# Chunked gate sums, split maximum rows and ScalarE head scaling in an mLSTM and ConvFFN decoder layer

## The chip, the cores and the metric

The kernel runs as one program on one core of a Trainium2 chip. TensorE (PE in the profile; PEld is its weight load), VectorE (DVE), ScalarE (ACT), GpSimd (POOL) and SyncE (SP, which only issues DMAs here) each have an instruction stream of their own and meet at semaphores. The metric is device time in microseconds, the median of several runs; lower is better.

## The reference, cut to what matters

One decoder layer on 512 positions of width 1024: a mixer (four mLSTM heads of width 256, beside a gated convolution of width 31 with a layer norm) and a convolutional FFN of inner width 2816. The change lies in the gates of the mLSTM and in the norm of its heads. For a head, with chunks of 128 positions:

```python
lfc = jax.nn.log_sigmoid(chunks(f_pre))
b = jnp.cumsum(lf_, axis=-1)
dmat = jnp.where(causal, b[..., :, None] - b[..., None, :] + i_[..., None, :], -jnp.inf)
m_t = jnp.maximum(b + m[..., None], jnp.max(dmat, axis=-1))
scores = jnp.einsum("bhtd,bhsd->bhts", q_, k_) * jnp.exp(dmat - m_t[..., None])
...
h = num / jnp.maximum(jnp.abs(den), jnp.exp(-m_t))[..., None]
...
h = rms_norm(h, ml_norm_g[l].reshape(H, Dh)).reshape(Bsz, S, D_ML)
```

The kernel carries no state from chunk to chunk. With F the running sum of the log forget gates over all 512 positions and a = i - F, the running maximum of a over positions (not below 0) is M, and the weight of source s at target t is exp(a_s - M_t).

## The kernel before

Positions lie as NT = 4 tiles of 128, channels as KT = 8 tiles of 128. Every large product runs in three passes of type float32r, high part by high, high by low and low by high (`mm3`, lines 198 to 202), 512 columns each. `w_load` brings a weight block by an SP DMA into one of two raw buffers and splits it into a high part on ACT (line 182) and a low part on POOL (line 183).

After the gated inputs and the first value product `make_v(0)`, which also gives the gates `gz`, the stretch of the change begins. The log forget gates `lf` are computed on ACT and DVE (lines 568 to 576). On TensorE then come, in the order of the code:

- the projections `qko` 0 and 1 of head 0 (`head_proj`, 24 matmuls each; 0 and 1 give q, 2 and 3 give k, 4 and 5 the output gate `so`),
- the running sums F in bank `fcum` (line 608): for tile tt one product with the triangle `tri` and one with `ones` for each earlier tile, ten float32 products of 4 columns; DVE copies F out as `Fc` (line 610) and forms `ga` = a (line 611),
- projection 2, then `aT` (line 616): a turned to 4 rows of 512 by products with `ident`; DVE scans the running maximum into `Mr` (line 618),
- projection 3, then `mtok` (line 623): the maximum turned back to positions, used in `em` (lines 625 and 626), and `make_E(0)`,
- projections 4 and 5.

`make_E(h)` (lines 588 to 599) spreads row h of `Mr` over 128 partitions by a float32 product into bank `Mb` (line 590), adds the causal mask on DVE (`Md`, line 592) and takes seven exponentials on ACT into `E` (lines 597 and 599); three of them read `Mb` itself.

Then, for heads 0 to 2, `attention(h)` is woven with the projections of head h + 1: scores `s` (line 514), their product with `E` on DVE (line 515), outputs `o` (line 525), copied and squared on ACT into `hn` and `ssq` (lines 528 to 530), the factor `fac` on DVE and POOL (lines 535 to 541), the scaling of `hn` by `fac` on DVE (line 544: four instructions per head), and the turn `hT` of the scaled heads on TensorE (line 550), which DVE and ACT use for the parts `hh` and `hl`. `make_E(h + 1)` and the values `v` of head h + 1 stand between `o` and `hT`. The banks of `fcum`, `aT`, `mtok`, `Mb`, `s`, `o` and `hT` are two PSUM buffers used in turn (`atbank`); the second bank of `hT` of a head is thus the one that `Mb` of the next head had.

Beside all this run the 31 taps of the convolution: 25 per channel tile on DVE (`cv`, line 716), the rest on ACT and POOL, and after the last tap the blocks of the conditioning weights (`ada`: a DMA issued from ACT's queue, line 165, and a product with a sum on DVE, line 167).

TensorE and SP issue in the order of the code. On DVE, ACT and POOL a scheduler merges the streams when the program is built, from times of its own model; the taps and the `ada` blocks have the lowest priority. Once built, each engine's order is fixed.

Of the kernel before, what the change touches and what calls it, by code (L numbers as in the profile page):

```python
# [10 lines left out]
F32 = mybir.dt.float32  # L11
F32R = mybir.dt.float32r
BF16 = mybir.dt.bfloat16
AF = mybir.ActivationFunctionType
ALU = mybir.AluOpType
PSUM = bass.MemoryType.PSUM

P = 128
D = 1024
T = 512  # L20
KT = D // P
NT = T // P
H = 4
# [31 lines left out]
def decoder_layer(ctx, tc, w_glu0, x, c, adaT, vecs, w_glu, w_qko, w_v0, w_v, w_out, w_up, w_down, out):  # L55
    nc = tc.nc
    V, S, G, PE = nc.vector, nc.scalar, nc.gpsimd, nc.tensor

    const = ctx.enter_context(tc.tile_pool(name="const", bufs=1))
# [28 lines left out]
    def slot(name, dt=F32):  # L88
        return slots.tile([P, T], dt, tag="t", name=name)
# [15 lines left out]
    ident = const.tile([P, P], F32, name="ident")  # L105
    make_identity(nc, ident)
    ones = const.tile([P, P], F32, name="ones")
    V.memset(ones, 1.0)
    tri = const.tile([P, P], F32, name="tri")
# [156 lines left out]
    for tt in range(NT):  # L266
# [9 lines left out]
        if tt < NT - 1:  # L276
# [7 lines left out]
                    op0=ALU.add)  # L284
# [204 lines left out]
    def head_proj(h, i):  # L489

        pieces, qs, ks, so = heads[h]
        ps = mmbank(f"qko{h}_{i}")
        proj(ps, pieces, i * KT)
        e = 2 * h + i % 2
        if i < 2:
            qs.append(conv4(ps, e, f"q{h}_{i}"))
        elif i < 4:
            ks.append(conv4(ps, 8 + e, f"k{h}_{i}"))
        else:
            t = slot(f"so{h}_{i}")  # L500
            S.activation(t, ps, AF.Tanh, scale=0.5)
            so.append(t)
# [3 lines left out]
    def attention(h):  # L506

        _, qs, ks, so = heads[h]

        for cc in range(NT):  # L510
            n = NS[cc]
            sp = atbank(f"s{h}_{cc}")
            for d in range(2):
                PE.matmul(sp[:, :n], ks[d][:, cc * P : (cc + 1) * P], qs[d][:, cc * P :], start=d == 0, stop=d == 1)  # L514
            V.scalar_tensor_tensor(out=E[h][cc], in0=sp[:, :n], scalar=DH**-0.5, in1=E[h][cc], op0=ALU.mult, op1=ALU.mult)
            if cc % 2:
                yield
        ssq = small.tile([P, NT], F32, tag="ssq", name=f"ssq{h}")
        dm = small.tile([P, NT], F32, tag="dm", name=f"dm{h}")
        hn = [slot(f"hn{h}_{i}") for i in range(2)]  # L520
        for tt in range(NT):
            o = atbank(f"o{h}_{tt}")
            for cc in range(tt + 1):
                a = (tt - cc) * P
                PE.matmul(o[:, : DH + 2], E[h][cc][:, a : a + P], vs[h][cc], start=cc == 0, stop=cc == tt)
            junk = small.tile([P, DH], BF16, tag="junk2", bufs=2, name=f"junko{h}_{tt}")
            hv = hn[tt // 2][:, (tt % 2) * DH : (tt % 2 + 1) * DH]
            S.activation(dm[:, tt : tt + 1], o[:, DH : DH + 1], AF.Abs)
            S.activation(hv, o[:, :DH], AF.Copy)
            S.activation(junk, hv, AF.Square, accum_out=ssq[:, tt : tt + 1])  # L530
            if tt in (1, 2):
                yield
        rd = small.tile([P, NT], F32, tag="rd", name=f"rd{h}")
        fac = small.tile([P, NT], F32, tag="fac", name=f"fac{h}")
        V.tensor_tensor(out=dm, in0=dm, in1=em[:, :, h], op=ALU.max)
        V.reciprocal(rd, dm)
        V.tensor_tensor(out=ssq, in0=ssq, in1=rd, op=ALU.mult)
        V.tensor_tensor(out=ssq, in0=ssq, in1=rd, op=ALU.mult)
        V.tensor_scalar(out=ssq, in0=ssq, scalar1=1.0 / DH, scalar2=EPS, op0=ALU.mult, op1=ALU.add)
        G.tensor_tensor(out=fac, in0=ssq, in1=mhalf, op=ALU.pow)  # L540
        V.tensor_tensor(out=fac, in0=fac, in1=rd, op=ALU.mult)
        for tt in range(NT):
            hv = hn[tt // 2][:, (tt % 2) * DH : (tt % 2 + 1) * DH]
            V.tensor_scalar(out=hv, in0=hv, scalar1=fac[:, tt : tt + 1], scalar2=None, op0=ALU.mult)
        yield
        for e in range(2):
            tp = atbank(f"hT{h}_{e}")
            for tt in range(NT):
                src = hn[tt // 2][:, (tt % 2) * DH + e * P : (tt % 2) * DH + (e + 1) * P]
                PE.transpose(tp[:, tt * P : (tt + 1) * P], src, ident)  # L550
            t = so[e]
            V.scalar_tensor_tensor(out=t, in0=t, scalar=1.0, in1=tp, op0=ALU.add, op1=ALU.mult)
            hi, lo = slot(f"hh{h}_{e}", F32R), slot(f"hl{h}_{e}", F32R)
            g = ghalf[:, 2 * h + e : 2 * h + e + 1]
            S.activation(hi, t, AF.Copy, scale=g)
            last_lo[0] = V.scalar_tensor_tensor(out=lo, in0=t, scalar=g, in1=hi.bitcast(F32), op0=ALU.mult, op1=ALU.subtract)
            hy[2 * h + e] = (hi, lo)
# [8 lines left out]
    fa, fe, fu, fl, fr, lf = (g16(f"g_{i}") for i in ("fa", "fe", "fu", "fl", "fr", "lf"))  # L566
# [18 lines left out]

    E = [None] * H

    def make_E(h):
        mb = atbank(f"Mb{h}")
        PE.matmul(mb, ident[:H, h : h + 1].to_broadcast([H, P]), Mr, start=True, stop=True)  # L590
        md = slot(f"Md{h}")
        V.tensor_tensor(out=md.rearrange("p (t m) -> p t m", t=NT), in0=mb.rearrange("p (t m) -> p t m", t=NT),
                        in1=cmask[:, None, :].to_broadcast([P, NT, P]), op=ALU.add)
        E[h] = head_tiles(f"E{h}", F32)
        for cc in range(NT):
            b = ga[:, cc, h : h + 1]
            S.activation(E[h][cc][:, :P], md[:, cc * P : (cc + 1) * P], AF.Exp, bias=b, scale=-1.0)
            if cc < NT - 1:
                S.activation(E[h][cc][:, P:], mb[:, (cc + 1) * P :], AF.Exp, bias=b, scale=-1.0)
# [3 lines left out]

    fps = atbank("fcum")
    fv = fps[:, : NT * H].rearrange("p (t h) -> p t h", t=NT)
    for tt in range(NT):
        for cc in range(tt + 1):
            PE.matmul(fv[:, tt, :], tri if cc == tt else ones, lf[:, cc, :], start=cc == 0, stop=cc == tt)
    Fc, ga = g16("Fc"), g16("ga")
    V.tensor_copy(Fc, fv)  # L610
    V.tensor_tensor(out=ga, in0=gz[:, :, :H], in1=Fc, op=ALU.subtract)
    head_proj(0, 2)

    aps = atbank("aT")
    for tt in range(NT):
        PE.matmul(aps[:H, tt * P : (tt + 1) * P], ga[:, tt, :], ident, start=True, stop=True)
    Mr = const.tile([H, T], F32, name="Mr")
    V.tensor_tensor_scan(out=Mr, data0=aps[:H, :], data1=zero[:H, :].to_broadcast([H, T]), initial=0.0, op0=ALU.max, op1=ALU.max)
    head_proj(0, 3)
    mps = atbank("mtok")  # L620
    mv = mps[:, : NT * H].rearrange("p (t h) -> p t h", t=NT)
    for tt in range(NT):
        PE.matmul(mv[:, tt, :], Mr[:, tt * P : (tt + 1) * P], ident[:H, :H], start=True, stop=True)
    em = g16("em")
    V.tensor_tensor(out=em, in0=Fc, in1=mv, op=ALU.add)
    S.activation(em, em, AF.Exp, scale=-1.0)

    make_E(0)
    for i in range(4, 6):
        head_proj(0, i)  # L630


    RD = float(D) ** 0.5
# [483 lines left out]
```

## Time and profile before

| | us |
|---|---|
| median of 3 runs | 800.17 |
| lowest and highest run | 799.45, 800.42 |
| span of the profiled execution, first to last instruction | 795.9 |
| TensorE busy in it | 781.6 |
| VectorE, GpSimd, ScalarE busy | 474.5, 436.5, 380.1 |
| idle time of TensorE before the heads' turn `hT` of head 0 | 1.4 |
| idle time of TensorE before `aT` | 0.7 |

The profile is of one execution; its own time is its span and some 4.3 us around it, as far as the median tells. Rows of a timeline give start, length, engine, line, operation and tile; a bracket at the end of a row is the idle time ahead of it and what ended that. Lengths overlap, since an engine starts the next instruction before the last has left it; the distance of two starts is what an instruction costs in a full queue.

### The profile page before, as it was taken

What the parts mean: (1) busy time and instruction counts of PE and PEld (TensorE: products, weight loads), DVE (VectorE), ACT (ScalarE), POOL (GpSimd) and SP (SyncE); (2) the same over time, 40 slices, a digit from 0 to 9 for tenths busy, and PEclk for the clock granted to TensorE, in tenths of its full rate; (3) what the DMA queues carried; (4) which work ended last, traced back from release to release, by engine and by line L of the source; (5) the groups of instructions that cost most, each with busy time, mean ns of one, the idle gap of its engine ahead of it and who ended that gap; (6) DMA issues with size and microseconds to landing.
All of it is one profiled execution on the core that took longest, in us unless ns stands there. A gap on an engine that the chain in (4) does not pass through costs nothing.

```text
span 795.9 us, 10370 instructions
## 1 busy us (share of the span) xinstructions
PE 781.6 (98%) x3786; PEld 652.2 (82%) x3786; DVE 474.5 (60%) x748; ACT 380.1 (48%) x709; POOL 436.5 (55%) x351
## 2 busy tenths in 40 slices
PE   7999999999999999999999999999999999999996
PEld 5888897777888888888889988888888888888885
DVE  6769999999996435547958794455444453000014
ACT  6684548758474454561345454444444444212212
POOL 4789759869598433442841474444454444444420
PEclk9999999999999999999999999999999999999998
DMA  8963214122037231426854652222222222222205
GB/s 326 347 243 133 81 61 153 54 105 107 28 94 250 80 133 55 159 106 235 320 187 157 218 180 106 106 75 84 106 106 106 105 90 97 107 105 106 80 0 186
DMA packets 24887, 106.97 MB, mean 134 GB/s; under 512 B 2914, under 2 KB 2946, under 8 KB 17412
## 3 DMA queue, kind: packets, MB, share of 16 engines
q1 hardware_dynamic: 16740, 83.22, 29.3%
q10 hardware_dynamic: 8096, 23.08, 8.2%
q8 instruction: 30, 0.49, 0.3%
q14 instruction: 21, 0.17, 0.1%
HBM read 102.08 MB, written 4.21 MB: 134 GB/s over the span
## 4 chain that ended last, share of the span: by engine, by line
PE 90%; DVE 5%; ACT 1%; DMA 1%; issue 1%; DVEq 0%; POOL 0%; SPq 0%; POOLq 0%; ACTq 0%
PE up L201 10%; PE up L200 10%; PE up L202 10%; PE dn L202 5%; PE dn L200 5%; PE dn L201 5%; PE qko L200 4%; PE qko L201 4%; PE qko L202 4%; PE glu L345 4%; DVE cv L716 3%; PE glu L200 2%; PE glu L201 2%; PE glu L202 2%; PE s L514 2%; PE mixa L202 2%
## 5 line engine op out<-in xcount | busy, mean ns | idle before, releaser
L716 DVE SCALAR_TENSOR_TENSOR cv<-gt,cvw,cv 128x502 f32<-128x502 f32 (+24 forms) x200 | 134.4, 725 | 1.9 <-ACT cv L704 1.3
L1043 DVE TENSOR_TENSOR fo<-dn,g2r 128x512 f32<-128x512 f32 x8 | 5.5, 692 | 100.3 <-PE dn L202 100.3
L712 POOL TENSOR_TENSOR cs<-cs,cs 128x510 f32<-128x510 f32 (+3 forms) x32 | 42.8, 1341 | 3.6 <-ACT cs L710 3.6
L183 POOL TENSOR_TENSOR wup_1024l<-wup,wup_1024h 128x512 fp32r<-128x512 f32 x20 | 27.0, 1348 | 31.8 <-ACT wup_1024h L182 31.7
L183 POOL TENSOR_TENSOR wup_1536l<-wup,wup_1536h 128x512 fp32r<-128x512 f32 x20 | 27.0, 1352 | 29.1 <-ACT wup_1536h L182 29.0
L183 POOL TENSOR_TENSOR wup_512l<-wup,wup_512h 128x512 fp32r<-128x512 f32 x20 | 26.8, 1338 | 23.4 <-ACT wup_512h L182 23.4
L183 POOL TENSOR_TENSOR wup_0l<-wup,wup_0h 128x512 fp32r<-128x512 f32 x20 | 27.2, 1358 | 20.8 <-ACT wup_0h L182 20.8
L201 PE MATMUL up<-u2l,wup_0h 128*128 128x512 f32 (+1 forms) x100 | 36.5, 365 | 0.2 <-DVE u2l L885 0.2
L200 PE MATMUL up<-u2h,wup_0h 128*128 128x512 f32 (+1 forms) x100 | 36.5, 365 | 0.0
L200 PE MATMUL up<-u2h,wup_1024h 128*128 128x512 f32 (+1 forms) x100 | 36.4, 364 | 0.0
L202 PE MATMUL up<-u2h,wup_0l 128*128 128x512 f32 (+1 forms) x100 | 36.4, 364 | 0.0
L200 PE MATMUL up<-u2h,wup_512h 128*128 128x512 f32 (+1 forms) x100 | 36.4, 364 | 0.0
L201 PE MATMUL up<-u2l,wup_512h 128*128 128x512 f32 (+1 forms) x100 | 36.4, 364 | 0.0
L202 PE MATMUL up<-u2h,wup_512l 128*128 128x512 f32 (+1 forms) x100 | 36.4, 364 | 0.0
L200 PE MATMUL up<-u2h,wup_1536h 128*128 128x512 f32 (+1 forms) x100 | 36.4, 364 | 0.0
L201 PE MATMUL up<-u2l,wup_1536h 128*128 128x512 f32 (+1 forms) x100 | 36.4, 364 | 0.0
L202 PE MATMUL up<-u2h,wup_1536l 128*128 128x512 f32 (+1 forms) x100 | 36.4, 364 | 0.0
L202 PE MATMUL up<-u2h,wup_1024l 128*128 128x512 f32 (+1 forms) x100 | 36.4, 364 | 0.0
L201 PE MATMUL up<-u2l,wup_1024h 128*128 128x512 f32 (+1 forms) x100 | 36.3, 363 | 0.0
L167 DVE SCALAR_TENSOR_TENSOR junk<-ada,cb 128x1024 bf16<-128x1024 f32 x20 | 32.6, 1631 | 6.3 <-DMA ada<-in_adaT 6.2
L183 POOL TENSOR_TENSOR wqko_1024l<-wqko,wqko_1024h 128x512 fp32r<-128x512 f32 x12 | 16.6, 1380 | 25.8 <-PE v L201 15.1
L183 POOL TENSOR_TENSOR wd_1024l<-wd,wd_1024h 128x512 fp32r<-128x512 f32 x11 | 14.3, 1296 | 29.8 <-ACT wd_1024h L182 29.8
(727 smaller groups left out, 2617.0 us busy)
## 6 DMA issues: line engine op xcount, KB each, us to landing
wup<-in_w_up SPq DMA_DIRECT2D x22, 1024.0 KB, 4.8
wqko<-in_w_qko SPq DMA_DIRECT2D x12, 1024.0 KB, 4.7
wd<-in_w_down SPq DMA_DIRECT2D x11, 1024.0 KB, 4.8
ada<-in_adaT ACTq DMA_DIRECT2D x20, 512.0 KB, 5.6
ada<-in_adaT SPq DMA_DIRECT2D x16, 512.0 KB, 7.6
wo<-in_w_out SPq DMA_DIRECT2D x8, 1024.0 KB, 4.7
spare<-in_adaT ACTq DMA_DIRECT2D x12, 512.0 KB, 8.4
wglu<-in_w_glu SPq DMA_DIRECT2D x5, 1024.0 KB, 8.3
```

What stands on the lines that cost most here:

```text
L167: t = V.scalar_tensor_tensor(out=junk, in0=r, scalar=1.0, in1=cb, op0=ALU.mult, op1=ALU.mult, accum_out=mod[:, i : i + 1])
L183: (eng or G).tensor_tensor(out=lo[:, :n], in0=src, in1=hi[:, :n].bitcast(F32), op=ALU.subtract)
L200: PE.matmul(ps, a[0], b[0], start=start, stop=False)
L201: PE.matmul(ps, a[0], b[1], start=False, stop=False)
L202: PE.matmul(ps, a[1], b[0], start=False, stop=stop)
L345: PE.matmul(ps, blk(wk, i)[a], u[k][b], start=k == 0 and p == 0, stop=k == KT - 1 and p == 1)
L514: PE.matmul(sp[:, :n], ks[d][:, cc * P : (cc + 1) * P], qs[d][:, cc * P :], start=d == 0, stop=d == 1)
L712: G.tensor_tensor(out=side[:, d:], in0=side[:, d:], in1=t[:, d:], op=ALU.add)
L716: last_tap = V.scalar_tensor_tensor(out=cp[:, d:], in0=cvx[j][:, : T - d], scalar=w(CK - 1 - d), in1=cp[:, d:], op0=ALU.mult, op1=ALU.add)
L1043: V.tensor_tensor(out=m, in0=banks[tt][hf], in1=g2r[hf], op=ALU.mult)
```

## The change

```diff
-            V.tensor_scalar(out=hv, in0=hv, scalar1=fac[:, tt : tt + 1], scalar2=None, op0=ALU.mult)
+            S.activation(hv, hv, AF.Copy, scale=fac[:, tt : tt + 1])
...
+    LO = 32
+    Mhl = const.tile([LO + H, T], F32R, name="Mhl")
+    G.memset(Mhl.bitcast(F32), 0.0)
+    pick = const.tile([LO + H, H], F32R, name="pick")
+    G.memset(pick.bitcast(F32), 0.0)
+    for a in (0, LO):
+        G.tensor_copy(pick[a : a + H, :], ident[a : a + H, a : a + H])
+
     def make_E(h):
         mb = atbank(f"Mb{h}")
-        PE.matmul(mb, ident[:H, h : h + 1].to_broadcast([H, P]), Mr, start=True, stop=True)
+        PE.matmul(mb, pick[:, h : h + 1].to_broadcast([LO + H, P]), Mhl, start=True, stop=True)
...
-    for tt in range(NT):
-        for cc in range(tt + 1):
-            PE.matmul(fv[:, tt, :], tri if cc == tt else ones, lf[:, cc, :], start=cc == 0, stop=cc == tt)
+    for d in range(NT):
+        PE.matmul(fv[:, d:, :], ones if d else tri, lf[:, : NT - d, :], start=d == 0, stop=d == NT - 1)
...
     head_proj(0, 2)
+    head_proj(0, 3)
 
     aps = atbank("aT")
     for tt in range(NT):
-        PE.matmul(aps[:H, tt * P : (tt + 1) * P], ga[:, tt, :], ident, start=True, stop=True)
-    Mr = const.tile([H, T], F32, name="Mr")
+        PE.transpose(aps[:H, tt * P : (tt + 1) * P], ga[:, tt, :], ident)
+    Mr = slot("Mr")[:H, :]
     V.tensor_tensor_scan(out=Mr, data0=aps[:H, :], data1=zero[:H, :].to_broadcast([H, T]), initial=0.0, op0=ALU.max, op1=ALU.max)
-    head_proj(0, 3)
+    V.tensor_copy(Mhl[:H, :], Mr)
+    V.tensor_tensor(out=Mhl[LO : LO + H, :], in0=Mr, in1=Mhl[:H, :].bitcast(F32), op=ALU.subtract)
+    head_proj(0, 4)
     mps = atbank("mtok")
...
-        PE.matmul(mv[:, tt, :], Mr[:, tt * P : (tt + 1) * P], ident[:H, :H], start=True, stop=True)
+        PE.transpose(mv[:, tt, :], Mr[:, tt * P : (tt + 1) * P], ident[:H, :H])
...
     make_E(0)
-    for i in range(4, 6):
-        head_proj(0, i)
+    head_proj(0, 5)
```

The sums F are formed by the distance d of chunks: one product with `tri` for all four tiles, then one with `ones` for each distance, four products of 16, 12, 8 and 4 columns. `aT` and `mtok` become transposes. `Mr` is split into a float32r high part in rows 0 to 3 of `Mhl` and the rest in rows 32 to 35, and one float32r product with `pick` (ones at rows h and 32 + h) spreads both; the rows between hold zeros. `aT` stands behind projection 3 now, `mtok` and `make_E(0)` behind projection 4. The heads' last scaling is an ACT instruction.

The scheduler builds another order on DVE, ACT and POOL from this. Three places of it follow; line numbers in the rows of the changed kernel are its own, higher by 7 to 10 than those before from line 596 on.

DVE from the scan of the maximum to `em`, before (`cv` are taps, `k_2c` and `k_3c` the short convolution of k):

```order
L618 SCALAR_TENSOR_TENSOR Mr<-aT,zero 4x512
L716 SCALAR_TENSOR_TENSOR cv_1674<-gt_832,cvw,cv_1674 128x505
L475 SCALAR_TENSOR_TENSOR k_2c<-qko_2_1270,vec,k_2c 128x511
L716 SCALAR_TENSOR_TENSOR cv_1625<-gt_761,cvw,cv_1625 128x499
L716 SCALAR_TENSOR_TENSOR cv_1674<-gt_832,cvw,cv_1674 128x504
L475 SCALAR_TENSOR_TENSOR k_2c<-qko_2_1270,vec,k_2c 128x510
L716 SCALAR_TENSOR_TENSOR cv_1625<-gt_761,cvw,cv_1625 128x498
L716 SCALAR_TENSOR_TENSOR cv_1674<-gt_832,cvw,cv_1674 128x503
L475 SCALAR_TENSOR_TENSOR k_2c<-qko_2_1270,vec,k_2c 128x509
L716 SCALAR_TENSOR_TENSOR cv_1625<-gt_761,cvw,cv_1625 128x497
L625 TENSOR_TENSOR em<-Fc,mtok 128x16
```

and the same stretch of the changed kernel:

```order
L626 SCALAR_TENSOR_TENSOR Mr<-aT,zero 4x512
L475 SCALAR_TENSOR_TENSOR k_3c<-qko_3_1301,vec,k_3c 128x511
L725 SCALAR_TENSOR_TENSOR cv_1676<-gt_832,cvw,cv_1676 128x504
L725 SCALAR_TENSOR_TENSOR cv_1627<-gt_761,cvw,cv_1627 128x497
L627 CAST Mhl<-Mr 4x512
L475 SCALAR_TENSOR_TENSOR k_3c<-qko_3_1301,vec,k_3c 128x510
L725 SCALAR_TENSOR_TENSOR cv_1676<-gt_832,cvw,cv_1676 128x503
L725 SCALAR_TENSOR_TENSOR cv_1627<-gt_761,cvw,cv_1627 128x496
L628 TENSOR_TENSOR Mhl<-Mr,Mhl 4x512
L475 SCALAR_TENSOR_TENSOR k_3c<-qko_3_1301,vec,k_3c 128x509
L635 TENSOR_TENSOR em<-Fc,mtok 128x16
```

The cast and the subtraction stand behind three other instructions each. Ahead of the scan, 5 instructions stood between it and `ga`; now it is 13 (five of q_1c and k_2c, eight taps). Up to the factor `fac` of head 0 the changed order has three taps fewer than before.

ACT ahead of the exponentials of head 2, beside the attention of head 1, before (`wqko_1_*h` are high parts of weights, `so` an output gate):

```order
L182 ACTIVATE wqko_1_0h<-wqko_1_2749 128x512
L182 ACTIVATE wqko_1_512h<-wqko_1_2749 128x512
L501 ACTIVATE so_5_2569<-qko_5_2544 128x512
L597 ACT_TABLE_LOAD
L597 ACTIVATE E_2575<-Md_2573,ga 128x128
L599 ACTIVATE E_2575<-Mb_2571,ga 128x384
```

and changed:

```order
L182 ACTIVATE wqko_1_0h<-wqko_1_2751 128x512
L544 ACTIVATE hn_0_2443<-hn_0_2443,fac_2534 128x256 x2
L544 ACTIVATE hn_1_2444<-hn_1_2444,fac_2534 128x256 x2
L182 ACTIVATE wqko_1_512h<-wqko_1_2751 128x512
L501 ACTIVATE so_5_2571<-qko_5_2546 128x512
L605 ACT_TABLE_LOAD
L605 ACTIVATE E_2577<-Md_2575,ga 128x128
```

The scaling, which waits for `fac`, stands ahead of a weight part, an output gate, the load of the table and the exponentials. For head 0 it stands behind the exponentials of head 1.

ACT where the weights of head 3 begin, before (`ada` are the DMAs of the conditioning weights):

```order
L182 ACTIVATE wqko_0_0h<-wqko_0_2731 128x512
L476 ACTIVATE k_2c<-k_2c 128x512
L165 DMA ada_3225<-in_adaT 128x1024
L728 ACTIVATE ydl_1816<-ydl_1816 128x512
L182 ACTIVATE wqko_0_512h<-wqko_0_2731 128x512
L473 ACTIVATE k_3c<-qko_3_2456,vec 128x512
```

and changed:

```order
L182 ACTIVATE wqko_0_0h<-wqko_0_2733 128x512
L476 ACTIVATE k_2c<-k_2c 128x512
L182 ACTIVATE wqko_0_512h<-wqko_0_2733 128x512
L473 ACTIVATE k_3c<-qko_3_2458,vec 128x512
L165 DMA ada_3227<-in_adaT 128x1024
```

The DMA of that block now stands behind a weight part and the start of `k_3c`.

## The prediction

> **What bounds the kernel now.** I read the page first, then TensorE's own waits, then busy time by stretch, then timelines around each line that the change touches.
>
> ```profile
> span 795.9 us, 10370 instructions
> PE 781.6 (98%) x3786; PEld 652.2 (82%) x3786; DVE 474.5 (60%) x748; ACT 380.1 (48%) x709; POOL 436.5 (55%) x351
> PE 90%; DVE 5%; ACT 1%; DMA 1%; issue 1%; DVEq 0%; POOL 0%; SPq 0%; POOLq 0%; ACTq 0%
> ...
> PE hT L550 <- DVE hn L544: 1.4, 1, 1.4
> PE aT L616 <- DVE ga L611: 0.7, 1, 0.7
> ```
>
> TensorE is busy for 98% of the span, and after the opening it waits in only two places that matter, both for VectorE and both in the part that is changed. So work taken from TensorE should come off the time one for one, unless a wait takes its place. The average hides that VectorE, idle for 40% of the span, is full exactly here. These rows give, for a stretch, its length and the busy time of PE, PEld, DVE, ACT and POOL:
>
> ```profile
> 117.00:143.00 26.00, 25.28 (x125) 20.48 (x123) 25.86 (x42) 20.03 (x34) 25.43 (x21) 1.00 0.37 126
> 143.00:170.00 27.00, 27.00 (x116) 20.95 (x117) 27.00 (x46) 17.36 (x32) 19.55 (x16) 1.00 0.20 74
> 170.00:229.00 59.00, 57.56 (x298) 47.82 (x297) 58.83 (x100) 38.69 (x80) 44.91 (x35) 1.00 0.20 72
> 229.00:260.00 31.00, 31.00 (x152) 25.69 (x151) 24.04 (x37) 16.50 (x37) 28.00 (x17) 1.00 0.69 223
> ```
>
> From 117 to 229 us VectorE works 111.7 of 112 us, mostly on taps that TensorE doesn't need yet. A result that TensorE does need comes when VectorE has worked through whatever stands ahead of it. Both waits of TensorE are of this kind.
>
> **What TensorE saves.**
>
> ```profile
> 116.73 0.39 PE L200 MATMUL qko<-uh,wqko_0h 128*128 128x512 f32 x1
> 127.61 0.28 PE L608 MATMUL fcum<-g_lf,tri 128*128 128x4 f32 x2
> 129.76 0.49 PE L200 MATMUL qko<-uh,wqko_0h 128*128 128x512 f32 x1
> ...
> 136.22 1.04 PE aT L616 x8
> 142.97 0.98 PE mtok L623 x8
> 254.62 1.05 PE Mb L590 x2
> 264.49 0.87 PE hT L550 x8
> ```
>
> The first two rows frame 48 float32r matmuls of 512 columns: 10.88 us, 0.227 each, 5.44 for a projection. A float32 product is two instructions, a transpose one (eight transposes of `hT` are x8).
>
> - `fcum`: 20 instructions in 2.15 us (127.61 to 129.76), 0.108 each; 8 remain: saves 1.29. More columns could make them dearer, at most as `aT`'s 0.13: then 1.11.
> - `aT`: eight at 0.13 become four at `hT`'s 0.11: saves 0.60. Behind one more projection `ga` is there in time: 0.72 of waiting goes.
> - `mtok`: half of 0.98, 0.49.
> - `Mb`: 1.05 becomes one float32r product, 0.23 by the projections' matmuls, 0.53 if it costs as one of the present pair: saves 0.52 to 0.82. I take 0.8, since its 512 columns are float32r like theirs. Four heads: 3.2.
> - `hT` of head 0 waits 1.44, which goes if the scaled heads come early.
>
> Together 1.29 + 0.60 + 0.72 + 0.49 + 3.2 + 1.44 = 7.7 us. That is the ceiling; the rest is what VectorE lets through. GpSimd's new memsets and copies fall in the opening, where it is idle, and cost nothing.
>
> **The first meeting: `Mb` of head 0.** This product now needs cast and subtraction too.
>
> ```profile
> 131.84 0.74 DVE L475 SCALAR_TENSOR_TENSOR q_1c<-qko,vec,q_1c 128x511 f32<-128x511 f32 x1
> 132.50 0.73 DVE L716 SCALAR_TENSOR_TENSOR cv<-gt,cvw,cv 128x504 f32<-128x504 f32 x1
> 135.16 1.01 DVE L611 TENSOR_TENSOR ga<-gz,Fc 128x16 f32<-128x16 f32 x1
> 139.50 1.20 DVE L618 TENSOR_TENSOR_SCAN Mr<-aT,zero 4x512 f32<-4x512 f32 x1
> 140.63 0.71 DVE L716 SCALAR_TENSOR_TENSOR cv<-gt,cvw,cv 128x505 f32<-128x505 f32 x1
> ...
> 134.85 1.28 POOL L183 TENSOR_TENSOR wqko_0l<-wqko,wqko_0h 128x512 fp32r<-128x512 f32 x1
> ```
>
> A tap or a step of q and k costs 0.65 (132.50 - 131.84), the scan 1.13. `ga`, with 16 columns, took 1.01 and ended as GpSimd's instruction did (134.85 + 1.28 = 136.13): an operation between SBUF operands can have to wait one out. In the new order `ga` starts some three instructions after 131.84, near 133.9, and ends near 134.8. Thirteen instructions (8.4) bring the scan to 143.2, its result to 144.3; three more (1.9) the cast to 146.2; three more, the subtraction. Neither is in the trace. For both together the lower bound is 0.9 (scaled from the taps, since 512 columns of a tap are 0.65 and a cast has one input), the upper 3.4 (one wait of 1.25 behind GpSimd for each); I take 2.2, since GpSimd is busy in 25.4 of the 26 us above. `Mhl` is there at 150.3 (149.0 to 151.5). TensorE reaches `Mb` after 127.61 + 0.86 + three projections with their changes of weights (16.5) + 0.44 + 0.49 = 145.9. It waits 4.4 us (3.1 to 5.6) where it waited for nothing, which takes back all that was saved up to there. Behind it stand projection 5 and all of TensorE's work; VectorE goes on with taps meanwhile.
>
> Such a pause can cost the clock. Busy time of PE and the granted clock in the opening:
>
> ```profile
> 14.00:16.00 2.00, 0.75 (x7) 1.00 1.02 410
> 16.00:18.00 2.00, 1.88 (x8) 0.72 1.03 409
> 18.00:20.00 2.00, 2.00 (x6) 0.50 1.04 390
> 20.00:22.00 2.00, 2.00 (x9) 0.92 1.00 314
> ```
>
> After a thin stretch the clock fell to half and came back: 2 x (0.28 + 0.50 + 0.08) = 1.7 us lost. The pause may cost 0 to 1.7. [...]
>
> **The second meeting: `hT` of head 0.**
>
> ```profile
> 206.96 0.15 DVE L541 TENSOR_TENSOR fac<-fac,rd 128x4 f32<-128x4 f32 x1
> 208.31 1.13 DVE L544 TENSOR_SCALAR hn<-hn,fac 128x256 f32<-128x256 f32 x4
> 208.79 1.46 PE L550 MATMUL hT<-ident,hn 128*128 128x128 f32 x8 [1.44 <-DVE hn L544]
> 264.05 0.93 ACT L465 ACTIVATE v<-v 128x256 f32<-128x256 f32 x3
> ```
>
> TensorE came here at 207.35. It now comes at 207.35 - 4.7 (all savings up to here, `Mb` of head 1 included) + 4.4 = 207.05, up to 1.7 later with the slow clock. `fac` stands behind three taps fewer (-1.9) and behind cast and subtraction (+2.2): 207.2 (205.9 to 208.4). On ACT the scaling needs four instructions of 256 columns; three like copies take 0.93, so four 1.2, the first 0.4. ACT waits for nothing else there (it is ahead of the third copy of `v`). `hT` starts near 207.8 and ends near 209.25 instead of 210.0: 0.75 gained, 0.35 if the clock dropped. I take 0.6, between -0.7 and 1.9. Nearly all of the first meeting's wait is thus without consequence: VectorE would have held `hT` anyway.
>
> **The third meeting: `hT` of head 1.** Its second bank is that of `Mb` of head 2, so it needs the exponentials that read it.
>
> ```profile
> 242.16 0.33 ACTq L165 DMA_DIRECT2D ada<-in_adaT  x1
> 248.81 1.55 DVE L167 SCALAR_TENSOR_TENSOR junk<-ada,cb 128x1024 bf16<-128x1024 f32 x1 [0.92 <-DMA ada<-in_adaT]
> 257.75 1.25 DVE L541 TENSOR_TENSOR fac<-fac,rd 128x4 f32<-128x4 f32 x1 [1.21 <-POOL fac L540]
> 259.03 2.13 DVE L544 TENSOR_SCALAR hn<-hn,fac 128x256 f32<-128x256 f32 x4
> 256.51 0.62 ACT L182 ACTIVATE wqko_512h<-wqko 128x512 fp32r<-128x512 f32 x1
> 257.03 0.58 ACT L501 ACTIVATE so<-qko 128x512 f32<-128x512 f32 x1
> 257.62 1.28 ACT L597 ACT_TABLE_LOAD   x1
> 261.79 0.40 ACT L597 ACTIVATE E<-Md,ga 128x128 f32<-128x128 f32 x1 [2.90 <-DVE Md L592]
> 263.51 0.36 ACT L599 ACTIVATE E<-Mb,ga 128x128 f32<-128x128 f32 x1
> 264.33 1.04 PE L550 MATMUL hT<-ident,hn 128*128 128x128 f32 x8
> ```
>
> Before, the bank was free at 263.87 and wanted at 264.77. With `fac` ready at 259.0 the exponentials began at 261.79, 2.8 later; weight part, gate and table load were done long before. Now they follow the scaling: 1.2 + 0.1 + 0.55 + 0.6 + 1.28 = 3.7 after `fac`, 0.9 later. `fac` itself hangs on a chain of `ada` blocks by DMA: the order moves one DMA behind two ACT instructions (243.9 instead of 242.16, up to +1.75), though the queues have room to make that up, busy for 0.69 of the stretch from 229 to 260 (above), and fewer small steps follow the last block (some -0.45). I take -0.2. The bank is free near 264.6, where TensorE, 0.6 + 0.8 early, wants it at 263.4. `hT` then ends at 265.0 instead of 265.2: of all gains 0.2 is left. Heads 2 and 3 scale long before their `hT`; behind this place only `Mb` of head 3 saves, 0.8.
>
> **Sum.** 0.2 + 0.8 = 1.0 us off the profiled execution: 794.9 of 795.9. The runs' median lies 4.3 above the span, outside of anything changed: 800.17 - 1.0 = 799.2.
>
> **Rivals.**
> 1. The bank of head 1 is free in time, since the `ada` chain is earlier by the 1.2 that are missing: 0.6 + 0.8 + 0.8 = 2.2 off, 798.0. For it: the last blocks wait for DMAs, not for work. Against it: the scaling sits ahead of the table load in any case.
> 2. VectorE runs further ahead than I count, so none of the three meetings holds: 7.7 off, 792.5. Against it: 111.7 of 112 us busy.
> 3. Slower: the displaced `ada` DMA lands 1.75 later and passes that on through `fac`, scaling, table load and exponentials, so that the bank comes at 266.5; `hT` ends 1.7 late, and with 0.8 regained the time is 801.1; if the pause of 3 us at `hT` also halves the clock, 802.8. It decides from a delay of 1.0 on.
>
> [...]
>
> **How the numbers follow.** Forecast 0.36 (own range 798.2 to 800.3), rival 1 0.22, rival 2 0.14, rival 3 0.28 (0.2 of that with the halved clock). About 0.2% (1.6 us) is what a measurement of this kernel can tell from no change. Faster than 798.6: rival 2 with 0.14, rival 1 with 0.19, the forecast's lower end with 0.06: 0.39. Slower than 801.8: rival 3 with the halved clock, 0.2, and 0.03 from the forecast's upper end: 0.23. Within: 0.38. The range reaches into rival 2 (where one meeting of three still holds) and takes in the dear end of rival 3: 795.0 to 803.0.
>
> **What would show it.** A wait of TensorE of 3 to 6 us before `Mb` of head 0, ended by VectorE's `Mhl`; the granted clock below 1.00 behind it or not; `hT` of head 0 starting near 207.8 behind ACT; in head 1 a wait inside `hT` for ACT's exponentials, which start 3.7 after `fac`; each `Mb` near 0.23. Wrong would be: no wait at `Mb` (then rival 2), VectorE idle before 225 us, or `hT` of head 1 with no wait (rival 1).

## The result, and the profile after

The changed kernel takes 807.55 us in the median of 4 runs (805.33 to 809.04), the kernel before 800.29 (799.45 to 802.26): the ratio is 1.0093, its 95% interval 1.0074 to 1.0112. It is slower by 7.3 us, outside of the range that was forecast. A run's time lies 1.7 us above its span (805.33 and 803.6 here), so the 4.3 between the median and the profiled span before is no fixed margin: both profiled executions were quicker than the median of their kernel, the one before by some 2.7 us and this one by 2.2. First the page of the changed kernel: span, busy times, the chain that ended last, and the waits of TensorE by what they waited for (total, times, longest).

```profile
span 803.6 us, 10328 instructions
PE 780.6 (97%) x3762; PEld 652.0 (81%) x3762; DVE 474.7 (59%) x734; ACT 387.1 (48%) x725; POOL 434.7 (54%) x355
PE 79%; DVE 12%; ACT 3%; DMA 2%; issue 2%; POOL 1%; DVEq 0%; POOLq 0%; ACTq 0%
...
PE Mb L598 <- DVE Mhl L628: 7.1, 1, 7.1
...
PE hT L550 <- ACT hn L544: 2.2, 1, 2.2
PE hT L550 <- ACT E L607: 1.5, 1, 1.5
```

VectorE's share of the chain went from 5% to 12%. The three waits are the three meetings of the prediction, each in the place that it named, and all larger than it said. The busy time of TensorE fell by only 1.0 us although 24 instructions are gone, since some of the rest ran at half clock and took longer. The same four stretches as before (length; busy time of PE, PEld, DVE, ACT, POOL; granted clock):

```profile
117.00:143.00 26.00, 26.00 (x122) 21.52 (x121) 25.87 (x44) 21.55 (x36) 25.39 (x21) 1.00 0.38 132
143.00:170.00 27.00, 19.87 (x73) 14.67 (x73) 24.52 (x35) 12.62 (x24) 17.79 (x15) 0.81 0.15 52
170.00:229.00 59.00, 56.56 (x286) 47.35 (x285) 57.31 (x91) 36.25 (x76) 38.16 (x30) 0.97 0.19 71
229.00:260.00 31.00, 31.00 (x141) 25.85 (x140) 26.12 (x39) 19.68 (x40) 27.30 (x18) 1.00 0.51 170
```

Up to 143 us all is as forecast and TensorE no longer waits. In the second stretch TensorE loses 7 us of work and a fifth of its clock, and VectorE, which was full before, is idle for 2.5 us; in the third it is idle for another 1.7 (0.2 before).

What TensorE saved is read from the starts of its rows:

```profile
127.13 0.29 PE L615 MATMUL fcum<-g_lf,tri 128*128 128x16 f32 x2
127.27 0.81 PE L615 MATMUL fcum<-g_lf,ones 128*128 128x12 f32 x6
127.94 0.49 PE L200 MATMUL qko<-uh,wqko_0h 128*128 128x512 f32 x1
...
138.97 0.60 PE L624 MATMUL aT<-ident,ga 128*4 128x128 f32 x4
139.32 0.48 PE L200 MATMUL qko<-uh,wqko_0h 128*128 128x512 f32 x1
...
202.55 0.50 PE L598 MATMUL Mb<-Mhl,pick 36*128 36x512 f32 x1
202.98 0.38 PE L200 MATMUL v<-wv_0h,uh 128*128 128x256 f32 x1
```

`fcum` takes 0.81 (127.94 - 127.13), 1.34 less than before; `aT` 0.35, 0.62 less; a spread of the maximum 0.43 instead of 1.05 (198.46 - 197.41), 0.62 less.

The ledger between the two profiled executions, from the starts of TensorE's rows and its waits: the opening is 0.5 shorter by chance; `fcum`, `aT`, `mtok` and the wait before `aT` save 3.2; the first `Mb` waits 7.1, and the clock is halved for 5.5 us of work behind it (2.5 lost: from the start of `Mb` twelve rows take 5.53, where the spread takes 0.43 and eleven like rows behind `aT` 2.61 at full clock); the turn of head 0 waits 0.8 more and is followed by 3.4 us at half clock and has to wait for ScalarE's four instructions one by one (2.0 in all); the turn of head 1 waits 1.5; four `Mb` save 2.5. That makes +7.7, as much as the spans differ by.

Now the first meeting in the changed kernel, VectorE and then GpSimd:

```profile
141.81 1.20 DVE L626 TENSOR_TENSOR_SCAN Mr<-aT,zero 4x512 f32<-4x512 f32 x1
144.88 4.81 DVE L627 CAST Mhl<-Mr 4x512 fp32r<-4x512 f32 x1
149.62 0.73 DVE L475 SCALAR_TENSOR_TENSOR k_3c<-qko,vec,k_3c 128x510 f32<-128x510 f32 x1
151.68 0.68 DVE L628 TENSOR_TENSOR Mhl<-Mr,Mhl 4x512 fp32r<-4x512 f32 x1
```

```profile
144.46 1.29 POOL L183 TENSOR_TENSOR wqko_1024l<-wqko,wqko_1024h 128x512 fp32r<-128x512 f32 x1
145.69 1.28 POOL L729 TENSOR_TENSOR gt<-gt,cs 128x512 f32<-128x512 f32 x1
146.92 1.28 POOL L183 TENSOR_TENSOR wqko_1536l<-wqko,wqko_1536h 128x512 fp32r<-128x512 f32 x1
148.14 1.27 POOL L721 TENSOR_TENSOR cs<-cs,cs 128x510 f32<-128x510 f32 x1
155.18 1.28 POOL L740 TENSOR_TENSOR ysum<-ysum,gt 128x512 f32<-128x512 f32 x1 [5.77 <-DVE cs L718]
```

The scan starts 1.4 earlier than forecast, yet `Mhl` is there at 152.36 instead of 150.3. The cast alone took 4.81 us for 512 columns of 4 rows. It began while GpSimd was in an instruction, saw three more of them start, and ended 0.28 after GpSimd had run out of work (148.14 + 1.27 = 149.41). The clock around it (PE's busy time and granted clock, by 1 us):

```profile
145.00:146.00 1.00, 0.37 (x5) 1.00 0.00 0
...
147.00:148.00 1.00, 0.00 (x0) 0.87 0.00 0
...
157.00:158.00 1.00, 1.00 (x3) 0.51 0.00 0
158.00:159.00 1.00, 1.00 (x6) 1.00 0.00 0
```

The clock halved 2.4 us after TensorE had stopped, and came back 5.5 us after it had gone on.

### The profile page after: what moved, and what is told of

It is laid out like the page before. It is cut to its first block, busy times and chain, and to the rows that moved or that the text cites. A ratio compares the mean times of both kernels' runs of the same rounds, so it can differ in the third digit from the quotient of the medians.

```text
span 803.6 us, 10328 instructions
## 1 busy us (share of the span) xinstructions
PE 780.6 (97%) x3762; PEld 652.0 (81%) x3762; DVE 474.7 (59%) x734; ACT 387.1 (48%) x725; POOL 434.7 (54%) x355
## 4 chain that ended last, share of the span: by engine, by line
PE 79%; DVE 12%; ACT 3%; DMA 2%; issue 2%; POOL 1%; DVEq 0%; POOLq 0%; ACTq 0%
PE up L201 10%; PE up L202 10%; PE up L200 10%; DVE cv L725 5%; PE dn L201 5%; PE dn L202 5%; PE dn L200 5%; PE qko L200 2%; PE qko L201 2%; PE qko L202 2%; PE glu L200 2%; PE glu L201 2%; PE glu L202 2%; PE mixa L200 2%; PE mixa L202 2%
## 5 line engine op out<-in xcount | busy, mean ns | idle before, releaser
L725 DVE SCALAR_TENSOR_TENSOR cv<-gt,cvw,cv 128x485 f32<-128x485 f32 (+21 forms) x200 | 134.0, 731 | 3.1 <-ACT cv L713 2.5
L167 DVE SCALAR_TENSOR_TENSOR junk<-ada,cb 128x1024 bf16<-128x1024 f32 x20 | 30.7, 1534 | 9.4 <-DMA ada<-in_adaT 9.3
```

Source lines behind the costliest of these rows:

```text
L167: t = V.scalar_tensor_tensor(out=junk, in0=r, scalar=1.0, in1=cb, op0=ALU.mult, op1=ALU.mult, accum_out=mod[:, i : i + 1])
L725: last_tap = V.scalar_tensor_tensor(out=cp[:, d:], in0=cvx[j][:, : T - d], scalar=w(CK - 1 - d), in1=cp[:, d:], op0=ALU.mult, op1=ALU.add)
```

## The experiments

The table gives, for each profiled execution, where TensorE starts the running sums, the scores of head 0 (s0), the turn of head 0 (hT0) and the scores of heads 1, 2 and 3, then the median of the runs and the ratio to the kernel before on the same chip with its interval. The starts differ by up to 2 us already at the sums (127.1 to 129.1), so stretches between columns are compared, not single columns. In the names, "late E" has the first `Mb` and its exponentials one projection later, "late blocks" has the `ada` blocks behind head 1, "sums alone" and "scaling alone" make only that part of the change; each is told below. Every edit also lets the scheduler build another order on VectorE, ScalarE and GpSimd, so a run shows its edit together with that order: with the scan twice, for one, `Md` follows `em` at once, and in the changed kernel three instructions later.

| run | sums | s0 | hT0 | s1 | s2 | s3 | median | ratio |
|---|---|---|---|---|---|---|---|---|
| before | 127.6 | 161.3 | 208.8 | 213.0 | 268.1 | 324.9 | 800.29 | |
| changed | 127.1 | 166.4 | 214.1 | 220.3 | 276.4 | 332.6 | 807.55 | 1.0093 (1.0074 to 1.0112) |
| changed, again | 127.5 | 165.9 | 213.6 | 219.7 | 276.0 | 332.1 | 805.27 | 1.0076 (1.0055 to 1.0098) |
| cast on ScalarE | 128.5 | 164.4 | 212.0 | 218.2 | 278.3 | 334.4 | 805.98 | 1.0071 (1.0049 to 1.0093) |
| scan twice | 127.9 | 163.3 | 210.7 | 216.8 | 278.3 | 334.5 | 808.09 | 1.0099 (1.0080 to 1.0118) |
| scaling on VectorE | 128.1 | 164.6 | 213.3 | 218.8 | 273.3 | 329.5 | 803.99 | 1.0050 (1.0034 to 1.0066) |
| no split | 127.9 | 158.1 | 205.1 | 209.8 | 269.2 | 326.0 | 798.19 | 0.9981 (0.9966 to 0.9995) |
| sums alone | 129.1 | 159.3 | 208.1 | 212.2 | 269.9 | 326.7 | 799.62 | 0.9995 (0.9979 to 1.0011) |
| scaling alone | 127.3 | 161.7 | 208.2 | 212.8 | 270.2 | 326.9 | 800.85 | 1.0016 (0.9999 to 1.0034) |
| late E | 127.6 | 157.6 | 206.8 | 213.5 | 274.6 | 330.7 | 803.22 | 1.0041 (1.0020 to 1.0061) |
| late blocks | 127.8 | 166.2 | 213.9 | 220.0 | 274.5 | 332.4 | 806.01 | 1.0089 (1.0068 to 1.0109) |
| late E and late blocks | 128.4 | 161.4 | 209.3 | 215.1 | 269.6 | 326.5 | 799.26 | 0.9995 (0.9981 to 1.0008) |
| no split, late blocks | 128.6 | 158.8 | 206.5 | 211.2 | 266.3 | 324.2 | 796.28 | 0.9956 (0.9939 to 0.9972) |

### Cast on ScalarE, and the scan twice

```diff
-    V.tensor_copy(Mhl[:H, :], Mr)
+    S.activation(Mhl[:H, :], Mr, AF.Copy)
```

> The changed kernel with the cast of the maximum's high part on ScalarE instead of VectorE; all else as changed. Theory A (the cast of 4x512 on VectorE, 4.81 us, is held up by GpSimd's back-to-back instructions, 3.6 of them, and makes most of the 7.1 us wait at the first Mb): ScalarE makes the cast in 0.4 to 0.6, the subtraction is done near 147, TensorE waits 1 to 2.5 us at the first Mb, the clock behind it stays at 1.00, and the time falls by 5.5 to 9 from the changed kernel's, to 798.5 to 802. Theory B (the loss is where cast and subtraction stand in VectorE's queue, behind taps): the wait stays above 5, the time above 804. Theory C (the loss is the scaling on ScalarE, at the heads' turns): the wait at Mb goes but the turns of heads 0 and 1 wait longer by as much, time above 804.

```diff
-    V.tensor_copy(Mhl[:H, :], Mr)
+    V.tensor_tensor_scan(out=Mhl[:H, :], data0=aps[:H, :], data1=zero[:H, :].to_broadcast([H, T]), initial=0.0, op0=ALU.max, op1=ALU.max)
```

> The changed kernel with the high part made by a second scan from the PSUM bank (float32r output) instead of a cast from SBUF; VectorE does it still, with 1.1 us of work. Theory A: this scan takes 1.1 to 1.2 like the first, since its large operand is in PSUM, though GpSimd is as busy; TensorE waits 1.5 to 3 us at the first Mb; time 798.5 to 802. Theory B: VectorE is held as long as before, wait above 5, time above 804. Theory C: as in the run with the cast on ScalarE, above 804.

The high part itself came as fast as theory A said: the cast took 0.63 on ScalarE, and the second scan cost 1.12 on VectorE beside a GpSimd as busy. TensorE's waits with the cast on ScalarE:

```profile
PE Mb L598 <- DVE Mhl L628: 4.0, 1, 4.0
...
PE hT L550 <- ACT E L607: 2.7, 1, 2.7
PE hT L550 <- ACT hn L544: 2.2, 1, 2.2
```

The pause at `Mb` is 3 us shorter in both runs (4.0 and 4.1), but above the 1 to 2.5 and 1.5 to 3 expected: the subtraction still stands behind three or four other instructions of VectorE, and took 1.68 and 1.39 beside GpSimd where the changed kernel's, with GpSimd idle, took 0.68. And the time did not fall by what the pause lost. From s1 to s2 these two runs need 60.0 and 61.5 us where the changed kernel needs 56.2 and the kernel before 55.1: what was won at `Mb` was lost in the turn of head 1. So neither A nor B holds for the total. C named the place of the loss, but not its reason.

### No split, and the scaling back on VectorE

`no split` takes the float32 product of `Mr` in `make_E` again and drops cast, subtraction, `Mhl` and `pick`; the second run undoes the scaling alone.

```diff
-        PE.matmul(mb, pick[:, h : h + 1].to_broadcast([LO + H, P]), Mhl, start=True, stop=True)
+        PE.matmul(mb, ident[:H, h : h + 1].to_broadcast([H, P]), Mr, start=True, stop=True)
```

> The changed kernel without the split: Mb from the float32 product of the unsplit maximum, as before; gate sums by distance, transposes, the move by one projection and the scaling on ScalarE stay. Theories A and B: no wait at the first Mb, each Mb 1.05 us again; 9.9 us of wait and half clock go, 2.4 of TensorE work come back, time 798 to 801. Theory C: the turns of heads 0 and 1 still wait for ScalarE by 2 us and more each with a clock drop, time above 802.

```diff
-            S.activation(hv, hv, AF.Copy, scale=fac[:, tt : tt + 1])
+            V.tensor_scalar(out=hv, in0=hv, scalar1=fac[:, tt : tt + 1], scalar2=None, op0=ALU.mult)
```

> The changed kernel with the heads' last scaling back on VectorE; the split stays. Theories A and B: the wait of about 7 us at the first Mb and the half clock stay, time 806 to 809. Theory C: the time falls to 803 or lower.

Without the split the stretch from the sums to s0 is 30.2 instead of 39.3: nine microseconds hang on the split. That kernel is a little faster than the one before, and would be faster by more, were it not for the turn of head 1 (the run below with late blocks shows it). Its rows there, ScalarE and then TensorE:

```profile
259.24 1.71 ACT L544 ACTIVATE hn<-hn,fac 128x256 f32<-128x256 f32 x4 [0.97 <-DVE fac L541]
260.97 1.28 ACT L597 ACT_TABLE_LOAD   x1
262.26 0.40 ACT L597 ACTIVATE E<-Md,ga 128x128 f32<-128x128 f32 x1
...
263.98 0.36 ACT L599 ACTIVATE E<-Mb,ga 128x128 f32<-128x128 f32 x1
```

```profile
261.12 0.60 PE L550 MATMUL hT<-ident,hn 128*128 128x128 f32 x4
264.39 0.66 PE L550 MATMUL hT<-ident,hn 128*128 128x128 f32 x4 [2.67 <-ACT E L599]
```

The first bank of the turn is written at 261.12, the second must wait until the last exponential has read it (264.34). With the scaling on VectorE and the split kept, the wait there is gone (54.5 from s1 to s2) though the pause at `Mb` is 4.9; that run lies between both expectations, at 804.0. Split and scaling each make a wait, and not in the same place. How much time the scaling costs beside the split is less certain: in this run's profile the cast took 1.15 and not 4.81, so the pause was shorter for another reason too.

### The sums alone, and the scaling alone

The first has `no split` and the scaling on VectorE together, the second is the kernel before with the one line of the scaling changed.

> The kernel before with the gate sums by distance, the transposes and the move by one projection; Mb by the float32 product and the scaling on VectorE as before. Theory D (three meetings: the split makes a new wait at the first Mb; VectorE's factor sets the turn of head 0; the chain of ada blocks sets the turn of head 1): TensorE is some 3.3 us ahead at the first scores, loses 2 to 3.5 of it in a longer wait at the turn of head 0 (the clock may halve behind it), and the rest in the turn of head 1; time 798 to 801. Rival (TensorE's saved work comes off the end): no wait over 2 us, 796 to 797.5.

> The kernel before with only the heads' last scaling on ScalarE. Theory D: the turn of head 0 starts 0.5 to 1 earlier, the exponentials of head 2 come 0.5 to 1.5 later behind the scaling, so that the turn of head 1 waits inside for them by 0.5 to 2 and the clock may halve; time 799.5 to 802.5. Rival (the scaling is harmless, the split made all of the loss): 798.5 to 799.5 and no wait at the turn of head 1.

Both times and both places came out as theory D said. The sums alone bring TensorE to s0 3.4 us sooner after the sums than before (30.3 against 33.7), and all of it is waited away: 2.7 at the turn of head 0, for VectorE, where 1.4 was waited before, and 2.3 in the turn of head 1. So only 1.2 is lost at the first of the two, less than the 2 to 3.5 expected, and 2.5 at the second. The scaling alone gains 1.1 in its own place (46.4 from s0 to hT0 instead of 47.5), gives 0.5 of it back inside the turn (4.7 from hT0 to s1 instead of 4.2), and waits 2.0 in the turn of head 1.

### The blocks behind head 1

The eight `ada` blocks are ordered behind the last low part of head 1, so that none stands ahead of the factor of head 1 on VectorE. Here in the run without the split, then in the kernel before, then in the changed kernel.

```diff
     for i in range(16, 24):
-        ada_block(i, last_tap)
+        ada_block(i, lo_of[1])
```

> The changed kernel without the split, and with the eight ada blocks ordered behind the last part of head 1 instead of behind the last tap, so that none stands ahead of the factor of head 1 on VectorE. Theory D: the wait of 2.7 in the turn of head 1 goes with the half clock behind it, so the stretch from the scores of head 1 to those of head 2 falls from 59.5 to 54.5 to 55.5 and the time from 798.2 to 793 to 795. Rival (the factor of head 1 is late for another reason: the attention's own work on VectorE and ScalarE): the wait stays, 797 to 799.

> The kernel before with only the ada blocks ordered behind the last part of head 1. Theory D: nothing waits for the factor of head 1 in the kernel before, so the move alone is worth nothing: 799.5 to 800.8, the turn of head 0 waits 1 to 2 as before. Rival (what the run without the split and with late ada blocks won comes from the move of the blocks): 796 to 798.

> The changed kernel with only the ada blocks ordered behind the last part of head 1. Theory D (the two places take back each other's gain): the pause at the first Mb stays at 4 to 7, the wait in the turn of head 1 is gone, the stretch from the scores of head 1 to those of head 2 is 54.5 instead of 56 to 61; time 801 to 805. Rival (the pause alone makes the whole loss): 806 to 808.

Without the split the wait in the turn of head 1 went, and the stretch from s1 to s2 fell from 59.5 to 55.1 as expected; the median fell by 1.9 only, to 796.28 where 793 to 795 was expected. About 1.1 of the difference reappears from s2 to s3, where a product `o` of head 2 waits 0.9 for ScalarE among the moved blocks. In the kernel before the move gains nothing, and even costs a little more than was expected (801.63, ratio 1.0020, 1.0007 to 1.0033): there is nothing to free. In the changed kernel it gains nothing either (806.01), against the 801 to 805 of theory D: the wait of 1.5 goes from the turn of head 1 (54.5 from s1 to s2), and the same 1.5 comes back in head 2 (57.9 from s2 to s3 instead of 56.2):

```profile
303.59 1.57 PE L526 MATMUL o<-v,E 128*128 128x258 f32 x6 [1.46 <-ACT hn L530]
```

### The first Mb one projection later

```diff
-    make_E(0)
     head_proj(0, 5)
+    make_E(0)
```

> The changed kernel with only the first Mb and its exponentials behind projection 5. Theory D: the pause at the first Mb falls below 2.5, TensorE is 4 to 8 us earlier at the scores of head 0, but waits longer in the turn of head 1 (2 us and more, with the half clock), so that 2 to 5 of it are left; time 801 to 805. Rival (the pause alone makes the whole loss): 798 to 800.

> The changed kernel with its split and its scaling on ScalarE, but with the first Mb and its exponentials behind projection 5 instead of ahead of it, and the ada blocks behind the last part of head 1. Theory D: the wait at the first Mb falls from 7.1 to 0.5 to 2, the clock stays, the turn of head 1 doesn't wait; what is left is the turn of head 0 (2 to 3 and perhaps a half clock); time 793 to 798. Rival (the cast's time on VectorE costs as much wherever TensorE stands): the delay comes back at the scores of head 0, above 801.

> The changed kernel once more. [...] Rival (the cast is held for as long as GpSimd has work, each time): 3.5 to 5 again.

With `late E` alone TensorE doesn't pause at the first `Mb` any more in the profiled execution, whose cast took 1.20. Against the fresh run of the changed kernel it is 8.4 us ahead at s0, 6.8 at hT0, 6.2 at s1, and 1.4 at s2. Its waits show where the rest went:

```profile
PE hT L550 <- ACT hn L544: 3.5, 1, 3.5
PE hT L550 <- ACT E L607: 3.1, 1, 3.1
```

With the blocks moved too, the span is 797.5 and the median 799.26, as fast as before, though not the 793 to 798 expected; a wait of 1.5 at `Mb` remained in that execution, whose cast took 3.69, and the clock was halved for 3.4 us behind it. The two moves together do more than each alone: from the 1.0076 and 1.0093 of the changed kernel, late E alone comes to 1.0041, late blocks alone to 1.0089, both to 0.9995. Most of what is gained at the first meeting stays only where the tie of the third is taken away as well.

The fresh run of the changed kernel repeats the pause of 7.1. Its scan started at 143.38, as forecast, so the cast began 1.6 later than in the first execution; it took 3.58, within the 3.5 to 5 of the rival, and again ended 0.28 after GpSimd's last instruction ahead of a gap. A cast shorter by 1.2 thus made the same pause.

### What the cast costs

`cast probe` adds casts of 4x512 to the run without the split, into a tile that nothing reads: two behind the scan and two near the end; both probes are single runs, read for the casts alone. The second probe has ten behind the scan, in turn from the maximum and from a constant; theory E there is that a cast which meets a GpSimd instruction ends with one of them, and not always with the first.

> The changed kernel without the split, with four added casts of 4x512 from a constant into a tile that nothing reads: two on VectorE right behind the scan of the maximum, where GpSimd works without a gap, and two near the end, behind the last but one output tile, where GpSimd has nothing. Theory A (a cast from SBUF to SBUF waits as long as GpSimd's instructions follow one another): the first two take 2 to 5 us each as far as GpSimd has no gap and end with a GpSimd instruction's end; the last two take 0.3 to 0.6. Rival (a cast of so few rows into float32r is dear by itself): all four take the same 3 to 5.

> The changed kernel without the split, with ten added casts of 4x512 behind the scan, in turn from the maximum and from a constant, into a tile that nothing reads. Theory E: those that meet a GpSimd instruction take from 0.5 to some 5, with ends 0.3 behind the end of a GpSimd instruction, whatever the source; those that meet none 0.43. Rival (the source matters: the maximum's casts are the long ones): the five from the maximum 3 to 5, the five from the constant below 1.6.

Both casts behind the scan took 0.6 to 0.8 in the first probe, beside a busy GpSimd, instead of theory A's 2 to 5, and the two near the end 0.43 each. So a cast is cheap by itself, and it isn't held as long as GpSimd has work, each time. The ten:

```profile
145.67 3.67 DVE L621 CAST probe<-Mr 4x512 fp32r<-4x512 f32 x1
151.21 0.41 DVE L621 CAST probe<-vec 4x512 fp32r<-4x512 f32 x1
...
156.40 1.55 DVE L621 CAST probe<-vec 4x512 fp32r<-4x512 f32 x1
159.16 0.43 DVE L621 CAST probe<-Mr 4x512 fp32r<-4x512 f32 x1
...
163.48 1.47 DVE L621 CAST probe<-Mr 4x512 fp32r<-4x512 f32 x1
...
172.78 0.41 DVE L621 CAST probe<-vec 4x512 fp32r<-4x512 f32 x1
```

Three classes: 0.41 with GpSimd idle (0.43 for one begun 0.2 before a GpSimd instruction ended), about 1.5 when one that had just begun had to end, 3.67 when three had to. The source doesn't decide: of the casts from the maximum one took 3.67, one 1.47 and three 0.41 to 0.43. What decides between one, three and four is not settled: with the same rows around it the cast took 4.81 and 3.58 in the two executions of the changed kernel, 3.57 with late blocks, 3.69 with late E and late blocks, but 1.20 with late E and 1.15 with the scaling on VectorE. It isn't where in GpSimd's instruction the cast begins: these six and the 3.67 all began 0.38 to 0.43 after one had started. The first four all ended 0.28 after GpSimd ran out of work, but the 3.67 ended with GpSimd's next instruction ready, so that is no rule either.

### Two attempts at a better kernel

The first is `no split, late blocks` with the last product of the factor on GpSimd; the second is the changed kernel with that, the scan twice, late E and late blocks.

```diff
-        V.tensor_tensor(out=fac, in0=fac, in1=rd, op=ALU.mult)
+        G.tensor_tensor(out=fac, in0=fac, in1=rd, op=ALU.mult)
```

> The run without the split and with late ada blocks, and with the last product of the heads' factor on GpSimd, behind its power there, instead of on VectorE behind six taps. Theory D: the factor of head 0 comes 1 to 2 earlier, the wait at the turn of head 0 falls from 1.6 to below 0.6; time 794 to 796. Rival (GpSimd's queue delays the factor as much as VectorE's did): 796 to 797.5.

> The changed kernel with its split and scaling on ScalarE, and four repairs: the high part by a second scan from PSUM, the first Mb behind projection 5, the ada blocks behind head 1, the factor's last product on GpSimd. Theory D: no wait at the first Mb, no half clock, waits below 1 at the turns; each Mb saves 0.55 against the run without the split; time 791.5 to 794.5. Rival (the split's work on VectorE comes back as a later factor of head 0): a wait of 2 or more there, above 796.

The first takes 795.91 (ratio 0.9953, 0.9939 to 0.9968): the wait at the turn of head 0 is down to 0.5, another in head 2 up to 1.4. It beats the kernel before by 3.7 us on the same chip and the changed one by more, and is not told apart from `no split, late blocks`. The second takes 797.91 (0.9977, 0.9966 to 0.9989), 3.4 over the top of what was expected. In its profile the first `Mb` no longer waits, but a score of head 0 waits 1.0 for the exponentials, the turn of head 0 waits 1.8 and is followed by half clock. So even the repaired split wins nothing over the float32 product that it replaces (2.0 more in the median, at the edge of what the two intervals tell apart).

## Why the prediction was wrong

**What TensorE saves: right.** 1.34, 0.62 and 0.51 for `fcum`, `aT` and `mtok` against 1.29, 0.60 and 0.49, and the wait before `aT` went. `Mb` saves 0.62, in the lower half of 0.52 to 0.82; 0.8 was taken.

**The first meeting: the mechanism right, the size wrong.** The wait stood where it was said, for `Mhl`, with the taps ahead of it. It was 7.1 instead of 4.4 (3.1 to 5.6). The term that was mis-sized is the cast: with the subtraction "one wait of 1.25 behind GpSimd for each" was taken as the worst, 3.4 together; both took 5.4, and 4.2 in the fresh run, where the scan came as forecast. One instruction can last until several of GpSimd's have ended: the cast of 4.81 until four had, the fresh run's 3.58 until three had. The clock cost 2.5 there, where 0 to 1.7 was allowed.

**The second meeting: the step that failed.** It said "Nearly all of the first meeting's wait is thus without consequence: VectorE would have held `hT` anyway", and before that "VectorE goes on with taps meanwhile". The factor was put at 207.2, counted as work alone. It came at 213.34. VectorE did not go on: it was in the cast itself for 4.7 us, and its fixed order has work among the taps that comes from TensorE by way of ScalarE. VectorE's waits, then the two instructions of ScalarE that stood ahead of what it waited for, then the factor:

```profile
DVE q_0c L475 <- ACT q_0c L473: 2.4, 1, 2.4
DVE cv L725 <- ACT cv L713: 1.2, 1, 1.2
...
166.41 0.63 ACT L182 ACTIVATE wqko_1536h<-wqko 128x512 fp32r<-128x512 f32 x1 [2.09 <-PE qko L201]
...
181.67 0.63 ACT L182 ACTIVATE wv_5h<-wv 128x512 fp32r<-128x512 f32 x1 [1.11 <-PE qko L201]
...
213.34 0.15 DVE L541 TENSOR_TENSOR fac<-fac,rd 128x4 f32<-128x4 f32 x1
```

Before, VectorE never waited there for more than 0.2. The same sum with what was measured: 206.96 before, three taps fewer (-1.9), cast and subtraction 5.4, 3.6 of new idle time, 214.1, against 213.34. The forecast had named the sign itself: "VectorE idle before 225 us". The runs bear the link out. Where TensorE pauses 4 us or more at the first `Mb` (the fresh run, late blocks, the cast on ScalarE, the scan twice, the scaling on VectorE), VectorE waits 1.4 to 2.0 at `q_0c`; where it pauses 1.5 or not at all (both runs with late E, no split, the sums alone), that wait is gone, and no other up to the last tap is longer than 1.0. A full engine had no room here to take up another's delay: part of TensorE's pause came back as VectorE's, and with the cast's own time it made the turn of head 0 late.

**The third meeting: right, and it is what ties the others.** The scaling does put more between the factor and the exponentials: 5.3 in the changed kernel, 4.3 without the split, 4.0 before:

```profile
265.66 1.25 DVE L541 TENSOR_TENSOR fac<-fac,rd 128x4 f32<-128x4 f32 x1 [1.21 <-POOL fac L540]
...
270.95 0.40 ACT L605 ACTIVATE E<-Md,ga 128x128 f32<-128x128 f32 x1
```

Here 0.9 more was forecast, 0.3 to 1.3 came. What was not seen is that this place takes back most of what is gained ahead of it, for the changed kernel with late E as for the sums alone: TensorE's lead of 8.4 at s0 is 1.4 at s2 with late E, the lead of 3.4 of the sums alone ends at nothing. The forecast had this for its own sum ("of all gains 0.2 is left") but used it only against gains. The factor of head 1 stands behind the last tap and the blocks, and these moved with VectorE: the last tap starts at 237.4 in the changed kernel, at some 228.3 before.

**The rivals.** The first, that the bank of head 1 is free in time, is excluded by the 1.5 waited there. The third had the right sign, and the right consequences of a late factor, but another cause for it: a displaced DMA of 1.75. The factor of head 1 was 7.9 late, and not by the blocks: from the first of them to the factor VectorE took 27.6 us (238.03 to 265.66) against 28.7 before, though it waited 3.7 for one DMA. TensorE was nearly as late, so that the wait it predicted at head 1 was only 1.5. The second rival, that none of the three meetings holds, is excluded: the changed kernel waits at all three in both executions.

**What stays open.** Why a cast waits for one GpSimd instruction in one execution and for three or four in another; and the exact division of the 7.3, since the meetings follow one another: the change without the scaling makes 1.0050, the scaling alone 1.0016, the change without the split 0.9981, and all of it 1.0076 to 1.0093.

## What to carry to other kernels

Ask of each new wait not only whether the engine behind it has slack, but whether the engine that is waited for has any: where two engines are both full and wait for each other in a fixed order, a pause of one can come back as a pause of the other (7.1 us on TensorE, 3.6 on VectorE here), and a gain on one alone can be waited away at the next meeting. Before a change that saves time on the busiest engine, list the meetings behind it in order and what each is tied to; take away the tie (here the order of the blocks) together with the work, or most of what is saved may be waited away. Work added on an engine that another is waiting for costs its place in the queue and what it waits for there, not only its own length (the cast: 0.41 alone, 4.81 in its place here).

## What was not expected of the hardware

A cast of 4x512 on VectorE between SBUF operands took 0.41 to 0.43 alone and up to 4.81 beside a busy GpSimd; a scan of the same size from PSUM took 1.12 to 1.13, start to start, in the same stretch. GpSimd's next instruction can be longer too: with the scaling on VectorE, where the cast took 1.15, it took 1.46 instead of 1.28. Beside the 4.81, three GpSimd instructions started while the cast was under way (145.69, 146.92 and 148.14), and none took longer than 1.28. Why the cast waits, and GpSimd after it, is not shown by any run here, only for how long.

The clock halved after some short pauses, and not after others: pauses of 1.5 (late E and late blocks) and 2.2 (changed, turn of head 0) were each followed by 3.4 us at half clock, pauses of 2.7 and 2.3 in the run of the sums alone by none. The rows around the 2.7:

```profile
206.00:207.00 1.00, 0.00 (x0) 1.00 0.00 0
207.00:208.00 1.00, 0.00 (x0) 1.00 0.00 0
208.00:209.00 1.00, 0.95 (x5) 1.00 0.00 0
209.00:210.00 1.00, 1.00 (x11) 1.00 0.00 0
```

Around the first meeting of the changed kernel the clock was halved for 10.2 us, from 147.7 to 158.0. The length of the pause alone does not decide, since 1.5 was followed by half clock and 2.7 was not; what does is not shown by any run here.
